# Output projection by seven products of quarters, its combined weight quarters made ready during the second segment

## The chip, the cores and the metric

The kernel runs on one core of a Trainium2 chip. The metric is the device time of one execution in microseconds (us); the times shown are those of three runs, and one more execution was profiled. The core's engines are called PE (matrix products, with PEld for its weight loads), DVE (vector), ACT (scalar and activation), POOL (GpSimd) and SP (here only the queue that issues transfers).

## The reference, cut to what matters

One layer: the input is normalised, multiplied by one wide input matrix, run through four branches (a gated convolution, gated linear attention, pooling windows, a state-space branch), the branches' outputs are set side by side as `mix` (2048 x 1024), and the layer ends with the part that is changed here:

```python
mix = jnp.concatenate([y_a, y_b, y_c, y_d], axis=-1)
x = x + mix @ w_out[layer]            # (2048 x 1024) @ (1024 x 1024)
...
return _rmsnorm(x, final_norm_w)
```

## The kernel before

The 2048 tokens are worked in two segments of 1024 (loop over `s`). Each segment computes its blocks of the input projection, the branches, and writes `mix`, transposed, to a scratch tensor `yd` in device memory (16 token tiles of 128 tokens, each 128 x 8 x 128). Every product is formed from split operands: `split` (L139, L140) makes a rounded high part on ACT and the remainder, the low part, on DVE; `mm3` (L186 to L188) then adds three products, high x low, high x high and low x high, over eight slices of the inner dimension, so one 128 x 512 output takes 24 matmuls. Accumulators come from a ring of three PSUM banks (`acc`), with two more banks tagged `up`.

The output projection follows the second segment. `load_wo` loads and splits the two column halves of the output matrix, half 0 during the last pooling blocks and half 1 at the start of the projection. Then, for each of the 16 token tiles, `load_y` loads a tile of `yd` and the residual input `xk` and splits the tile, `project` computes one column half in 24 matmuls, adds the residual on DVE (L796), and squares the sum on ACT for the row's mean square (L797; L799 and L801 gather it), and `emit` runs the reciprocal root on DVE (`rsqrt`, L127 to L135), scales the row by it and by the norm weight (L807), and stores it (L808). The last tile's second half is done in two pieces of 256 columns, and its output in three pieces, so that less is left to do when PE ends.

All transfers are issued by SP, one queue in program order; each issue waits in place until its buffer is free and its source is ready. The order of the instructions on each engine is set by the framework's scheduler; code that is queued with `later(n, fn)` is written out n blocks later, in `step()`.

Of the kernel before, what the change touches and what calls it, by code (L numbers as in the profile page):

```python
# [52 lines left out]
@with_exitstack  # L53
def tile_hybrid_trunk(ctx: ExitStack, tc: tile.TileContext, xtok, xT, wkv, wch, wpu, wz, wo, pw_, nw, par, gw, fnw, out):
    nc = tc.nc
    vec, act, pe, sp = nc.vector, nc.scalar, nc.tensor, nc.sync
# [207 lines left out]
    def later(n, fn):  # L264

        queue.append([n, fn])
# [246 lines left out]
    wout = []

    def load_wo(n):
        hi, lo = big(n)
        for i in range(4):
            raw = pw.tile([P, 2, 512], F32, tag="raw", name=nm("raw"), bufs=3)
            sp.dma_start(raw, wo[n, i])
            split(raw, hi[:, 2 * i:2 * i + 2, :], lo[:, 2 * i:2 * i + 2, :])  # L520
        wout.append((hi, lo))

# [78 lines left out]
    for s in range(NSEG):  # L601
# [170 lines left out]
    tiles = {}

    def load_y(tt):
        yr = pw.tile([P, KD, P], F32, tag="raw", name=nm("yr"), bufs=3)
        sp.dma_start(yr, yd[tt])
        yh = pw.tile([P, KD, P], F32R, tag="wh", name=nm("yh"))
        yl = pw.tile([P, KD, P], F32R, tag="wl", name=nm("yl"))
        split(yr, yh, yl)
        xk = px.tile([P, D], F32, tag="xtok", name=nm("xk"))  # L780
        sp.dma_start(xk, xtok[tt])
        r = px.tile([P, D], F32, tag="xT", name=nm("r"))
        ot = pseg.tile([P, D], F32, tag=("q", "kt")[tt % 2], name=nm("ot"))
        sq = psm.tile([P, 4], F32, tag="sq", name=nm("sq"))
        tiles[tt] = (yh, yl, xk, r, ot, sq)

    def project(tt, c0, c1, i):

        yh, yl, xk, r, ot, sq = tiles[tt]
        hi, lo = wout[c0 // 512]  # L790
        wc = slice(c0 % 512, c0 % 512 + c1 - c0)
        cs = slice(c0, c1)
        o = acc()[:, :c1 - c0]
        mm3(o, [(yh[:, k, :], yl[:, k, :], hi[:, k, wc], lo[:, k, wc]) for k in range(KD)])
        step()
        vec.tensor_tensor(r[:, cs], o, xk[:, cs], ALU.add)  # L796
        act.activation(xk[:, cs], r[:, cs], AF.Square, accum_out=sq[:, i:i + 1])  # L797
# [14 lines left out]
    load_wo(1)
    for n in range(2):
        for tt in range(2):
            project(tt, n * 512, (n + 1) * 512, n)
            if n == 1:
                emit(tt)
    for tt in range(2, NTT):
        load_y(tt)
        for i, (c0, c1) in enumerate(((0, 512), (512, 1024)) if tt < NTT - 1 else ((0, 512), (512, 768), (768, 1024))):  # L820
            project(tt, c0, c1, i)
        emit(tt)


def _pack(x, norm_w, w_in, conv_a_w, gla_gate_w, gla_gate_b, gla_norm_w, pool_w, pool_scale, ssd_conv_w, ssd_conv_b,
          ssd_dt_bias, ssd_a_log, ssd_d, ssd_norm_w, w_out, final_norm_w):

    f = np.float32
    c = np.ascontiguousarray
    x0 = np.asarray(x)[0]  # L830
    a = {}
    a['xtok'] = c(x0.reshape(SEQ // P, P, D))
    a['xT'] = c(x0.reshape(SEQ // HALF, HALF, KD, P).transpose(0, 3, 2, 1))
    w = np.asarray(w_in)[0]
# [7 lines left out]
    a['wo'] = c(np.asarray(w_out)[0].reshape(4, 2, P, 2, 512).transpose(3, 0, 2, 1, 4))  # L842
# [58 lines left out]
```

## Time and profile before

| | us |
|---|---|
| median of 3 runs (lowest, highest) | 828.62 (828.38, 830.47) |
| the profiled execution | 828.5 |
| its span, first to last instruction | 826.7 |
| PE busy in the span | 815.3 |
| DVE busy in the span | 499.2 |
| ACT busy in the span | 277.2 |
| POOL busy in the span | 3.1 |

The span is what the trace covers; 1.8 us of the profiled execution lie outside it. PE is busy for 99% of the span at a granted clock of 0.996, so times on the other engines count only where PE waits for them, and behind PE's last matmul.

### The profile page before, as it was taken

The numbers are of one execution on the slowest core, as the hardware profiler recorded it, in microseconds if no ns is written. First come the engines' busy times: TensorE is split into PE (matmuls) and PEld (weight loads), VectorE is DVE, ScalarE is ACT, GpSimd is POOL, SyncE is SP. The second block draws the span as 40 slices with busy tenths as digits, with TensorE's granted clock in tenths as the row PEclk, the third lists the DMA queues.
The fourth block names the chain that finished last, engine by engine and source line by source line (L and its number), as shares of the span: only waits on it lengthen the run. The fifth ranks groups of instructions, "written<-read, shape, count | busy, mean of one in ns | idle before, by whom it ended". The sixth has DMA issues, their size and how long they took to land.

```text
span 826.7 us, 11204 instructions
## 1 busy us (share of the span) xinstructions
PE 815.3 (99%) x4304; PEld 676.9 (82%) x4304; DVE 499.2 (60%) x1253; ACT 277.2 (34%) x491; POOL 3.1 (0%) x18
## 2 busy tenths in 40 slices
PE   8999999999999999999999999999999999999996
PEld 7988888787878888998888778788888888888885
DVE  6678576665554679946555453643668665545544
ACT  5755442341222413445454111122323422221211
POOL 0000000000000000000000000000000000000000
PEclk9999999999999999999999999999999999999999
DMA  8840210353330324430111011120146553343221
GB/s 280 320 154 25 77 52 26 107 191 119 92 88 1 122 74 146 147 103 27 52 51 52 27 58 45 52 62 16 55 157 198 177 184 134 142 153 128 102 102 52
DMA packets 38133, 85.66 MB, mean 104 GB/s; under 512 B 3680, under 2 KB 17344, under 8 KB 38080
## 3 DMA queue, kind: packets, MB, share of 16 engines
q1 hardware_dynamic: 38080, 84.95, 30.7%
q8 instruction: 34, 0.56, 0.3%
q14 instruction: 19, 0.16, 0.1%
HBM read 67.11 MB, written 17.83 MB: 103 GB/s over the span
## 4 chain that ended last, share of the span: by engine, by line
PE 97%; DMA 1%; DVE 1%; SPq 0%; ACT 0%; issue 0%; DVEq 0%; ACTq 0%
PE acc L186 30%; PE acc L188 29%; PE acc L187 29%; PE up L398 1%; PE oy L406 1%; PE up L581 1%; PE tr L649 1%; PE oy L410 1%; PE acc L581 1%; DMA xT<-in_xT 1%; DMA raw<-in_wkv 1%; PE oy L581 1%; PE up L394 1%; PE tr L166 0%; PE tr L211 0%; PE tr L708 0%
## 5 line engine op out<-in xcount | busy, mean ns | idle before, releaser
L186 PE MATMUL acc<-bl,wh 128*128 128x512 f32 x640 | 253.8, 397 | 0.0
L188 PE MATMUL acc<-bh,wl 128*128 128x512 f32 x640 | 249.8, 390 | 0.0
L187 PE MATMUL acc<-bh,wh 128*128 128x512 f32 x640 | 249.4, 390 | 0.0
L188 PEld LDWEIGHTS acc<-bh,wl 128*128 128x128 f32 x640 | 120.1, 188 | 25.5
L186 PEld LDWEIGHTS acc<-bl,wh 128*128 128x128 f32 x640 | 120.2, 188 | 25.1
L187 PEld LDWEIGHTS acc<-bh,wh 128*128 128x128 f32 x640 | 120.3, 188 | 23.6
L187 PE MATMUL acc<-bh,yh 128*128 128x512 f32 (+1 forms) x264 | 101.0, 383 | 0.0
L188 PE MATMUL acc<-bh,yl 128*128 128x512 f32 (+1 forms) x264 | 101.0, 383 | 0.0
L186 PE MATMUL acc<-bl,yh 128*128 128x512 f32 (+1 forms) x264 | 101.0, 383 | 0.0
L139 ACT CAST wh<-raw 128x1024 fp32r<-128x1024 f32 (+3 forms) x57 | 55.8, 980 | 121.8 <-PE acc L187 112.9
L140 DVE TENSOR_TENSOR wl<-raw,wh 128x1024 fp32r<-128x1024 f32 (+3 forms) x57 | 64.5, 1134 | 39.0 <-ACT wh L139 35.8
L186 PE MATMUL acc<-wl,bh 128*128 128x512 f32 (+1 forms) x192 | 69.1, 360 | 0.0
L188 PE MATMUL acc<-wh,bl 128*128 128x512 f32 (+1 forms) x192 | 68.4, 356 | 0.0
L187 PE MATMUL acc<-wh,bh 128*128 128x512 f32 (+1 forms) x192 | 68.4, 356 | 0.0
L383 DVE SCALAR_TENSOR_TENSOR g<-g,prm,g 128x512 f32<-128x512 f32 x72 | 53.6, 749 | 6.7 <-ACT g L381 5.2
L187 PEld LDWEIGHTS acc<-bh,yh 128*128 128x128 f32 x264 | 49.6, 188 | 9.8
L186 PEld LDWEIGHTS acc<-bl,yh 128*128 128x128 f32 x264 | 49.6, 188 | 9.7
L188 PEld LDWEIGHTS acc<-bh,yl 128*128 128x128 f32 x264 | 49.6, 188 | 9.6
L796 DVE TENSOR_TENSOR r<-acc,xk 128x512 f32<-128x512 f32 (+1 forms) x33 | 22.3, 675 | 57.1 <-PE acc L188 55.8
L797 ACT ACTIVATE xk<-r 128x512 f32<-128x512 f32 (+1 forms) x33 | 20.3, 616 | 87.0 <-issue 66.7
L186 PEld LDWEIGHTS acc<-wl,bh 128*128 128x128 f32 x192 | 36.1, 188 | 5.2 <-issue 0.3
L188 PEld LDWEIGHTS acc<-wh,bl 128*128 128x128 f32 x192 | 36.1, 188 | 5.1
(195 smaller groups left out, 880.7 us busy)
## 6 DMA issues: line engine op xcount, KB each, us to landing
raw<-in_wch SPq DMA_DIRECT2D x36, 512.0 KB, 3.4
xk<-in_xtok SPq DMA_DIRECT2D x24, 512.0 KB, 3.7
yr<-yd SPq DMA_DIRECT2D x16, 512.0 KB, 4.2
out<-ot SPq DMA_DIRECT2D x30, 256.0 KB, 2.4
xT<-in_xT SPq DMA_DIRECT2D x14, 512.0 KB, 4.6
xtok<-in_xtok SPq DMA_DIRECT2D x8, 512.0 KB, 4.6
raw<-in_wz SPq DMA_DIRECT2D x8, 512.0 KB, 3.8
yd<-g SPq DMA_DIRECT2D x16, 256.0 KB, 3.0
```

The lines of the kernel that those rows point to most:

```text
L139: act.copy(hi, raw)
L140: vec.tensor_sub(lo, raw, hi.bitcast(F32))
L186: pe.matmul(o, lhsT=lh, rhs=rl, start=i == 0, stop=False)
L187: pe.matmul(o, lhsT=lh, rhs=rh, start=False, stop=False)
L188: pe.matmul(o, lhsT=ll, rhs=rh, start=False, stop=i == last)
L383: vec.scalar_tensor_tensor(t, xin[:, k:k + 512], pcol('scw', 4 * i + k), t, ALU.mult, ALU.add)
L394: pe.matmul(o[h * 32:(h + 1) * 32, 0:CH], lhsT=kt[r, tt, h * 32:(h + 1) * 32], rhs=kv[r, tt, h * CH:(h + 1) * CH], start=True, stop=True)
L398: pe.matmul(o[:, CH + g * P:CH + (g + 1) * P], lhsT=bt[r, tt, g, :], rhs=wxs[r, tt, g * P:(g + 1) * P], start=True, stop=True)
L406: pe.matmul(oy[rows[i], 0:256], lhsT=q[:, tok[i]], rhs=st[i][0], start=True, stop=True)
L581: pe.matmul(o[tt][:, :KVN], lhsT=a[:, k, sl], rhs=wk[0][k][b], start=k == 0 and i == 0, stop=k == KD - 1 and i == 2)
L796: vec.tensor_tensor(r[:, cs], o, xk[:, cs], ALU.add)
L797: act.activation(xk[:, cs], r[:, cs], AF.Square, accum_out=sq[:, i:i + 1])
```

## The change

The 16 token tiles are taken in eight pairs. A pair's left factor is cut into four quarters (two token tiles by two halves of the inner dimension), the output matrix too (two halves of the inner dimension by two column halves), and the pair's four 128 x 512 outputs are formed from seven products of quarters in place of eight, with sums of quarters as factors. A product takes 12 matmuls of 512 columns (`mm12`).

- **Weights.** `wout_sums` forms four combined weight quarters on DVE, in place, and stores them to a scratch tensor `td`. `wq_load` loads each of the seven weight quarters (four from `td`) and splits it; b11, t2, b21, t1 and t3 go into segment tiles that are free by then and into the buffers of the first half of the input, t4 and b22 into those of the second half while the first pair is computed.
- **Left factors.** `prep7` splits seven quarters for each pair and forms the four sums s1 to s4 on POOL. It is advanced by one step behind each product.
- **Products and outputs.** `first7` forms a = a11 b11; `second7` puts its negative into a second accumulator b on ACT; `pair7` adds the other six products to a, b and a bank e, and reads b out twice on the way (`cp2`, `cp3`). The seven are, in PE's order, a11 b11 (ahead of the pair), s2 t2, a12 b21, s1 t1, s3 t3, a22 t4 and s4 b22; the next pair's a11 b11 stands between s3 t3 and a22 t4.
- **Order.** From the projection on, every engine keeps the order of the program text (`Ordered`, `strict`).

```diff
+    def wout_sums(g):
...
+            vec.tensor_sub(b11, b11, b12)
+            vec.tensor_sub(b12, b12, b22)
+            vec.tensor_add(b22, b22, b11)
+            vec.tensor_sub(b21, b21, b22)
+            for i, x in enumerate((b11, b22, b12, b21)):
+                sp.dma_start(td[i, :, 2 * g:2 * g + 2, :], x)
+        later(1, go)
+    def wq_load(n, hi, lo):
...
+        for g in range(2):
+            raw = px.tile([P, 2, HALF], F32, tag="xtok", name=nm("wq"))
+            sp.dma_start(raw, src[:, 2 * g:2 * g + 2, :])
+            split(raw, hi[g], lo[g])
+            yield 1
+    def prep7(raw, w7, n=0):
+        a11, a12, a21, a22, s1, s2 = raw
...
+        put('a11', a11)
+        pool.tensor_add(s1, a21, a22)
+        pool.tensor_add(s2, s1, a11)
+        pool.tensor_add(a21, a21, a11)
+        yield 1
+        put('a12', a12)
+        yield 1
+        put('s2', s2)
+        pool.tensor_add(s2, s2, a12)
+        yield 1
+        for n, r in (('s1', s1), ('s3', a21), ('a22', a22), ('s4', s2)):
+            put(n, r)
+            yield 1
+    def second7():
+        b = acc()
+        act.activation(b, ahead[0][0], AF.Copy, scale=-1.0)
+        ahead[0][1] = b
+    def pair7(w7, ev11, ev21, d12, d22, cp2, cp3, done, after=None):
+        a, b = ahead[0]
+        mm12(b, w7['s2'], Hw['t2'], False)
+        cp2(d12, b)
+        tick()
+        mm12(a, w7['a12'], Hw['b21'], False)
+        ev11(a)
+        tick()
+        e = ps_up.tile([P, 512], F32, tag="up", name=nm("e"))
+        mm12(e, w7['s1'], Hw['t1'], True)
+        tick()
+        mm12(b, w7['s3'], Hw['t3'], False)
+        cp3(d22, b)
+        vec.tensor_sub(d22, d22, e)
+        done(0)
+        tick()
+        if after is not None:
+            after()
+            tick()
+        mm12(b, w7['a22'], Hw['t4'], False)
+        if after is not None:
+            second7()
+        ev21(b)
+        done(1)
+        tick()
+        mm12(e, w7['s4'], Hw['b22'], False)
+        vec.tensor_sub(d12, e, d12)
+        done(2)
+        tick()
...
+            if j == 0:
+                later(1, lambda: square(self.r[1][1], self.sq[1], 0))
+            elif j == 1:
+                later(2, lambda: emit(self.tt + 1, self.rows[1], self.sq[1]))
+            else:
+                later(1, lambda: square(self.r[0][1], self.sq[0], 1))
+                later(3 if self.tt + 2 < NTT else 1, lambda: emit(self.tt, self.rows[0], self.sq[0]))
```

PE up to the start of the projection keeps its order. The first rows of the projection before are groups of 24 (here the heads of the first two; `yh`, `yl` are a token tile's parts, `bh`, `bl` the matrix half's):

```order
L186 MATMUL acc_5636<-bl_5444,yh_5598 128x512 [waits DVE_49,Activation_49]
L187 MATMUL acc_5636<-bh_5443,yh_5598 128x512
L188 MATMUL acc_5636<-bh_5443,yl_5599 128x512 [waits DVE_49]
...
L186 MATMUL acc_5664<-bl_5444,yh_5609 128x512 [waits Activation_49]
L187 MATMUL acc_5664<-bh_5443,yh_5609 128x512
```

After the change these are PE's rows of the last two pairs, the head of each product: the end of the pair of tiles 12 and 13 (acc_6691 is its b, e_6785 its e, acc_6832 the next pair's a), then the pair 14 and 15 (acc_6859 is its b, e_6944 its e):

```order
L75 MATMUL acc_6832<-wq_5258,wh_5581 128x512 [waits Activation_49]
...
L75 MATMUL acc_6691<-bh_5694,wh_5736 128x512 [waits DVE_49]
...
L75 MATMUL e_6785<-bl_5695,wh_5581 128x512 [waits DVE_49]
...
L75 MATMUL acc_6859<-wq_5487,wh_5590 128x512 [waits Activation_49]
...
L75 MATMUL acc_6832<-bh_5491,wh_5590 128x512 x2
...
L75 MATMUL e_6944<-bl_5492,wh_5696 128x512 x2
...
L75 MATMUL acc_6859<-wq_5490,wh_5696 128x512 [waits DVE_49,Activation_49]
...
L75 MATMUL acc_6859<-bh_5694,wh_5736 128x512 [waits DVE_49,Activation_49]
...
L75 MATMUL e_6944<-bl_5695,wh_5736 128x512 [waits DVE_49,Activation_49]
```

The pair 12 and 13 has the next pair's product ahead of a22 t4 (the second head); in the last pair a22 t4 (the last head but one) follows s3 t3 directly, on the same bank b, which DVE reads between the two.

DVE in a middle pair, from the last product of the pair of tiles 0 and 1 (r_5721 and r_5722 are its rows) to `cp3`, the second reading of b (acc_5851) in the pair 2 and 3; the splits write `wl`:

```order
L75 TENSOR_TENSOR r_5721<-e_5769,r_5721 128x512 [waits PE_49]
L75 TENSOR_TENSOR wl_5697<-raw_5575,wh_5696 128x512 [waits DMAHW4_49,Activation_49]
L75 TENSOR_SCALAR na_5875<-sq_5689 128x1 [waits DVE_49]
...
L75 SCALAR_TENSOR_TENSOR r_5722<-r_5722,ny_5874,g_5691 128x512
L75 SCALAR_TENSOR_TENSOR sq_5688<-sq_5688 128x1 [waits Activation_49]
L75 SCALAR_TENSOR_TENSOR r_5893<-acc_5851,g_5794 128x512 [waits DMAHW0_49,PE_49]
L75 TENSOR_TENSOR wl_5697<-raw_5580,wh_5696 128x512 [waits Activation_49]
L75 TENSOR_TENSOR r_5893<-acc_5824,g_5788 128x512 [waits DMAHW7_49,PE_49]
L75 TENSOR_TENSOR wl_5737<-raw_5574,wh_5736 128x512 [waits DMAHW4_49,Activation_49]
L75 TENSOR_SCALAR na_5931<-sq_5688 128x1 [waits DVE_49]
...
L75 SCALAR_TENSOR_TENSOR r_5721<-r_5721,ny_5930,g_5691 128x512
L75 TENSOR_TENSOR wl_5737<-raw_5574,wh_5736 128x512 [waits DMAHW5_49,Activation_49]
L75 TENSOR_TENSOR r_5894<-acc_5851,g_5794 128x512 [waits DMAHW2_49,PE_49]
```

Two whole tiles are emitted between the two ends, and four splits.

The end of DVE's program, before:

```order
L796 TENSOR_TENSOR r_6837<-acc_6896,xk_6835 128x256 [waits PE_49]
L801 SCALAR_TENSOR_TENSOR sq_6839<-sq_6839 128x1 [waits Activation_49]
L127 TENSOR_SCALAR na_6925<-sq_6839 128x1 [waits DVE_49]
...
L807 SCALAR_TENSOR_TENSOR ot_6838<-r_6837,ny_6924,fw 128x384 [waits DMAHW7_49,DMAHW0_49,DVE_49]
L807 SCALAR_TENSOR_TENSOR ot_6838<-r_6837,ny_6924,fw 128x320 x2
```

and after (r_6898 is tile 15's row, r_6897 tile 14's):

```order
L75 TENSOR_TENSOR r_6897<-e_6944,r_6897 128x512 [waits PE_49]
L75 TENSOR_SCALAR na_7006<-sq_6809 128x1 [waits DVE_49]
...
L75 SCALAR_TENSOR_TENSOR r_6898<-r_6898,ny_7005,g_5690 128x512 [waits DVE_49]
L75 SCALAR_TENSOR_TENSOR r_6898<-r_6898,ny_7005,g_5691 128x512
L75 SCALAR_TENSOR_TENSOR sq_6808<-sq_6808 128x1 [waits Activation_49]
L75 TENSOR_SCALAR na_7021<-sq_6808 128x1 [waits DVE_49]
...
L75 SCALAR_TENSOR_TENSOR r_6897<-r_6897,ny_7020,g_5690 128x512 [waits DVE_49]
L75 SCALAR_TENSOR_TENSOR r_6897<-r_6897,ny_7020,g_5691 128x512
```

One whole tile is emitted behind the last product before the last row's own emission.

## Rows read from the trace of the kernel before

**Rows 1.** The page: busy time of each engine, and the chain that ended last.
```profile
PE 815.3 (99%) x4304; PEld 676.9 (82%) x4304; DVE 499.2 (60%) x1253; ACT 277.2 (34%) x491; POOL 3.1 (0%) x18
PE 97%; DMA 1%; DVE 1%; SPq 0%; ACT 0%; issue 0%; DVEq 0%; ACTq 0%
```

**Rows 2.** Busy time by stretch: pooling blocks, projection, end (columns as headed).
```profile
core 0: us, PE busy (x) PEld busy (x) DVE busy (x) ACT busy (x) POOL busy (x), PEclk, DMA share, GB/s
600.00:645.00 45.00, 45.00 (x208) 37.41 (x207) 35.11 (x72) 13.70 (x22) 0.00 (x0) 1.00 0.51 164
644.78:819.30 174.52, 174.52 (x793) 145.34 (x791) 91.66 (x234) 40.70 (x83) 0.00 (x0) 1.00 0.38 134
819.30:826.70 7.40, 0.03 (x1) 0.00 (x0) 3.57 (x13) 0.51 (x2) 0.00 (x0) 0.80 0.20 71
```

**Rows 3.** Timeline of PE: a group's end and the next's start; 256-column matmuls.
```profile
698.96 0.39 PE L188 MATMUL acc<-bh,yl 128*128 128x512 f32 x1
699.18 0.39 PE L186 MATMUL acc<-bl,yh 128*128 128x512 f32 x1
...
813.42 0.28 PE L186 MATMUL acc<-bl,yh 128*128 128x256 f32 x1
813.54 0.28 PE L187 MATMUL acc<-bh,yh 128*128 128x256 f32 x1
```

**Rows 4.** Timeline behind that group: residual, square, and one tile's emission.
```profile
699.38 0.69 DVE L796 TENSOR_TENSOR r<-acc,xk 128x512 f32<-128x512 f32 x1 [3.76 <-PE acc L188]
700.12 0.63 ACT L797 ACTIVATE xk<-r 128x512 f32<-128x512 f32 x1
...
701.38 0.15 DVE L801 SCALAR_TENSOR_TENSOR sq<-sq 128x1 f32<-128x1 f32 x1
701.57 0.15 DVE L127 TENSOR_SCALAR na<-sq 128x1 int32<-128x1 int32 x1
...
703.30 1.41 DVE L807 SCALAR_TENSOR_TENSOR ot<-r,ny,fw 128x512 f32<-128x512 f32 x2
```

**Rows 5.** Groups by form: half splits, copies out of PSUM, POOL's largest.
```profile
L140 DVE TENSOR_TENSOR bl<-hf,bh 128x512 fp32r<-128x512 f32 x16 | 10.8, 687 | 0.8 <-ACT bh L139 0.7
L139 ACT CAST bh<-hf 128x512 fp32r<-128x512 f32 x16 | 9.9, 621 | 17.0 <-DVE hf L259 16.8
L381 ACT ACTIVATE g<-acc,prm 128x512 f32<-128x512 f32 x12 | 9.4, 784 | 0.0
L222 ACT COPY g<-acc 128x512 f32<-128x512 f32 x20 | 11.6, 582 | 20.9 <-PE acc L188 17.4 <-issue 3.6
L305 POOL MEMSET rst<- 96x512 f32 x4 | 2.0, 522 | 325.3 <-DVE g L499 323.0 <-DVE g L509 2.3
```

**Rows 6.** Timeline of the end.
```profile
819.37 0.42 DVE L796 TENSOR_TENSOR r<-acc,xk 128x256 f32<-128x256 f32 x1 [1.72 <-PE acc L188]
822.29 1.54 DVE L807 SCALAR_TENSOR_TENSOR ot<-r,ny,fw 128x384 f32<-128x384 f32 x3
```

**Rows 7.** Transfers: issues, KB of each, median us from issue to landing.
```profile
raw<-in_wo SPq DMA_DIRECT2D x8, 512.0 KB, 3.7
out<-ot SPq DMA_DIRECT2D x30, 256.0 KB, 2.4
out<-ot SPq DMA_DIRECT2D x2, 160.0 KB, 1.9
```

**Rows 8.** Groups of the projection: a whole weight split on ACT and DVE.
```profile
L139 ACT CAST bh<-raw 128x1024 fp32r<-128x1024 f32 x8 | 8.2, 1049 | 13.4 <-PE acc L186 8.4 <-DMA raw<-in_wo 4.9
L140 DVE TENSOR_TENSOR bl<-raw,bh 128x1024 fp32r<-128x1024 f32 x8 | 9.6, 1221 | 1.3 <-ACT bh L139 1.2
```

**Rows 9.** Timeline of DVE at the start of the second segment.
```profile
353.01 0.68 DVE L307 TENSOR_TENSOR rst<-tr,rst 16x512 fp32r<-16x512 f32 x1 [1.89 <-ACT rst L306]
360.75 2.38 DVE L140 TENSOR_TENSOR wl<-raw,wh 128x1024 fp32r<-128x1024 f32 x2 [7.06 <-ACT wh L139]
...
373.09 0.17 DVE L379 COPY halo_x<-g 128x3 f32<-128x3 f32 x1 [2.47 <-ACT g L222]
379.29 1.23 DVE L140 TENSOR_TENSOR wl<-raw,wh 128x1024 fp32r<-128x1024 f32 x1 [2.68 <-ACT wh L139]
```

More of the change, by code (lines that the diff above doesn't have):

```diff
@@ L21 @@
 KD = D // P
+KH = KD // 2
 CH = 64
@@ L55, in tile_hybrid_trunk, with __init__, __getattr__, call @@
     nc = tc.nc
-    vec, act, pe, sp = nc.vector, nc.scalar, nc.tensor, nc.sync
+    strict = [False]
+    class Ordered:
+        def __init__(self, eng):
+            self.eng, self.last = eng, None
+        def __getattr__(self, name):
+            def call(*args, **kw):
+                f = getattr(self.eng, name)
+                if not strict[0]:
+                    self.last = None
+                    return f(*args, **kw)
+                if self.last is None:
+                    r = f(*args, **kw)
+                else:
+                    with tc.issue_after(self.last):
+                        r = f(*args, **kw)
+                self.last = r.ins
+                return r
+            return call
+    vec, act, pe, sp, pool = [Ordered(e) for e in (nc.vector, nc.scalar, nc.tensor, nc.sync, nc.gpsimd)]
     cp = ctx.enter_context(tc.tile_pool(name="cp", bufs=1))
@@ L511, in pool_z, with go @@
         spill(s, f, 4 + j, sz)
[L513 to L521, printed above, removed]
+    Hw = {}
+    prep_, side = [None], [None]
+    def wout_sums(g):
+        t = {}
+        for q, tag in (((0, 0), "xT"), ((1, 0), "xT"), ((0, 1), "xtok"), ((1, 1), "xtok")):
+            t[q] = px.tile([P, 2, HALF], F32, tag=tag, name=nm("wo"))
+            sp.dma_start(t[q], wo[q[0], q[1], :, 2 * g:2 * g + 2, :])
+        def go():
+            b11, b12, b21, b22 = t[0, 0], t[1, 0], t[0, 1], t[1, 1]
+            vec.tensor_sub(b11, b11, b12)
[5 more added lines that the diff above has]
+        later(1, go)
@@ new lines, in tile_hybrid_trunk, with slot, load7 @@
+    rings = dict(wh=[0, [], F32R, 4], wl=[0, [], F32R, 4], raw=[0, [], F32, 3])
+    def slot(tag):
+        r = rings[tag]
+        i, n = r[0], r[3]
+        r[0] += 1
+        if i < 2 * n and i % 2 == 0:
+            r[1].append(pw.tile([P, 1024], r[2], tag=tag, name=nm(tag), bufs=n))
+        return r[1][i // 2 % n][:, i % 2 * 512:(i % 2 + 1) * 512]
+    def load7(tt):
+        raw = [slot("raw") for _ in range(4)]
+        for t, (a, b) in ((tt, raw[0:2]), (tt + 1, raw[2:4])):
+            sp.dma_start(a, yd[t][:, 0:KH, :].rearrange("p k n -> p (k n)"))
+            sp.dma_start(b, yd[t][:, KH:KD, :].rearrange("p k n -> p (k n)"))
+        return raw + [slot("raw") for _ in range(2)]
@@ new lines, in prep7, with put @@
+    def prep7(raw, w7, n=0):
+        a11, a12, a21, a22, s1, s2 = raw
+        def put(n, r):
+            w7[n] = slot("wh"), slot("wl")
+            split(r, *w7[n])
+        for _ in range(n):
+            yield 1
[11 more added lines that the diff above has]
+            put(n, r)
+            yield 1
@@ new lines, in tick, with chain, mm12 @@
+    def tick():
+        for g in (prep_, side):
+            if g[0] is not None and next(g[0], 0) == 0:
+                g[0] = None
+        step()
+    def chain(*gs):
+        for g in gs:
+            yield from g
+    def mm12(o, w, h, start):
+        (wh, wl), (hh, hl) = w, h
+        for k in range(KH):
+            ks = slice(k * P, (k + 1) * P)
+            for i, (a, b) in enumerate(((wh, hl), (wh, hh), (wl, hh))):
+                pe.matmul(o, lhsT=a[:, ks], rhs=b[k], start=start and k == 0 and i == 0,
+                          stop=k == KH - 1 and i == 2, skip_group_check=True)
@@ new lines, in tile_hybrid_trunk, with first7 @@
+    ahead = [None]
+    def first7(w7):
+        a = acc()
+        mm12(a, w7['a11'], Hw['b11'], True)
+        ahead[0] = [a, None]
+    def second7():
[31 more added lines that the diff above has]
+        tick()
@@ L764, in tile_hybrid_trunk, with store, square @@
                 pool_z(s, j, f, block_ch(f, wp[j][1]), ab)
+                if f == 1 and s + 1 == NSEG:
+                    for _ in range(4):
+                        next(rest)
+                    if j == 0:
+                        w7 = {}
+                        prep_[0] = prep7(load7(0), w7)
+                        for _ in range(4):
+                            next(prep_[0])
                 if f == 1 and s + 1 < NSEG:
                     wk[0] = load_kv((0, 1)) if j == 0 else wk[0] + load_kv((2,))
-    fw = pseg.tile([P, D], F32, tag="kv", name="fw")
-    sp.dma_start(fw, fnw.to_broadcast([P, D]))
-    vec.tensor_single_scalar(fw, fw, 1.0 / RS, ALU.mult)
+    while queue:
+        step()
     NTT = SEQ // P
[L772 to L797, printed above, removed]
+    def store(dst, src):
+        later(1, lambda: sp.dma_start(dst, src))
+    def square(r, sq, i):
+        junk = px.tile([P, HALF], F32, tag="hf", name=nm("junk"))
+        act.activation(junk, r, AF.Square, accum_out=sq[:, i:i + 1])
         if i == 0:
@@ L812, in tile_hybrid_trunk @@
[L812 to L822, printed above, removed]
+        for c in range(2):
+            cs = slice(c * 512, (c + 1) * 512)
+            vec.scalar_tensor_tensor(r[:, cs], r[:, cs], rs, fw[c], ALU.mult, ALU.mult)
+            store(out[tt, :, cs], r[:, cs])
@@ new lines, in tile_hybrid_trunk @@
+    rows = Rows(0)
+    fw = [gen()[:, :512] for _ in range(2)]
+    for c in range(2):
+        sp.dma_start(fw[c], fnw[:, c * 512:(c + 1) * 512].to_broadcast([P, 512]))
+    q5 = big(1)
+    strict[0] = True
+    next(prep_[0])
+    next(prep_[0])
+    side[0] = chain(wq_load('t4', halves(q5[0][:, 0:4, :]), halves(q5[0][:, 4:8, :])),
+                    wq_load('b22', halves(q5[1][:, 0:4, :]), halves(q5[1][:, 4:8, :])))
+    later(4, lambda: [act.activation(t, t, AF.Copy, scale=1.0 / RS) for t in fw])
@@ new lines, in tile_hybrid_trunk @@
+    first7(w7)
+    second7()
+    for tt in range(0, NTT, 2):
+        w_next = {}
+        nxt = []
+        if tt + 2 < NTT:
+            prep_[0] = chain(prep_[0] or (), prep7(load7(tt + 2), w_next))
+            later(3, lambda: nxt.append(Rows(tt + 2)))
+        rows.take()
+        pair7(w7, rows.ev11, rows.ev21, rows.r[0][1], rows.r[1][1], rows.cp2, rows.cp3, rows.done,
+              after=(lambda: first7(w_next)) if tt + 2 < NTT else None)
+        w7 = w_next
+        rows = nxt[0] if nxt else None
@@ L825, in _pack @@
+    while queue:
+        tick()
 def _pack(x, norm_w, w_in, conv_a_w, gla_gate_w, gla_gate_b, gla_norm_w, pool_w, pool_scale, ssd_conv_w, ssd_conv_b,
```

62 lines of the change are left out of this document (52 added, 10 removed).

## The prediction, on record before the result

> **What bounds the kernel now.** I read the page first: PE is busy for 815.3 of 826.7 us, and the chain that ended last is PE for 97% [rows 1]. So I looked at the stretch the change touches, by windows: from 644.78 to 819.30, the whole output projection, PE is busy without a gap at full clock while DVE works 91.7 us and ACT 40.7 [rows 2]. There the other engines have room, and what counts is how many matmuls PE issues and at what spacing. The timeline gives the spacing by starts, not by the 0.39 us that each row lasts (they overlap): 698.96 to 699.18, and 0.12 us for the 256-column ones [rows 3]. The projection has 31 groups of 24 wide matmuls (744) and two of 24 narrow ones (48 x 0.12 = 5.8), so a wide one takes (174.5 - 5.8) / 744 = 0.2268 us. Last I read what follows PE's last matmul: 7.40 us [rows 2], of which 2.87 lie behind the last vector operation (822.29 + 1.54 = 823.83) [rows 6].
>
> **The matmuls removed.** Eight pairs of seven products of 12 matmuls are 672 wide ones: 672 x 0.2268 = 152.4 against 174.5, **-22.1 us**. A product takes 2.72 us and a pair 19.05. The number of columns and the spacing stay, so this is the firmest term.
>
> **Can DVE and ACT feed it?** A pair now asks DVE for 7 splits, 6 readings of PSUM or of e and 4 scalings, 17 operations of about 0.69, and two short chains: 11.7 + 2 x 1.73 + some 0.6 = 15.8 of 19.05 us. A chain and its two scalings take 703.30 - 701.57 = 1.73 and 1.41, so 3.14 [rows 4], a half split 0.69 [rows 5]. The sum fits, but DVE keeps the program's order now, so I follow the dangerous stretch: from the end of s4 b22 (call it 0) to `cp3`, behind which a22 t4 waits. DVE starts 0.20 us behind PE (699.18 to 699.38 [rows 3, 4]); then e's reading, the a22 split, one emission, `cp2`, the s4 split, the reading of a, the next a11 split, another emission, the a12 split, `cp3`: 8 x 0.69 + 2 x 3.14 + 2 x 0.19 (from L801's start to L127's) = 12.2. It ends at 12.4 (it may not begin before s3 t3 ends, 10.9, which it does not). PE wants bank b at 5 x 2.72 = 13.6, since the next pair's a11 b11 covers one product. **1.1 us to spare**, a price of 0 without disturbance. If that product were not between, as in the last pair, the same wait is open: 0.20 + 0.69 + some 0.06 (DVE's 0.69 from 699.38 ends at 700.07, ACT follows at 700.12 [rows 4]) = **+0.95**, once. `cp2` has two products of cover, the e bank likewise, each split at least one. ACT does 7 casts of 0.62, a copy of 0.58 [rows 5] and 4 squares of 0.63 [rows 4] with their sums in a pair, under 9 us.
>
> **POOL's adds.** No row before has POOL adding. The nearest is a memset of 512 columns, 0.52, which only writes [rows 5]. Below I take 0.52; above, three such passes (two read, one written), 1.57; I take two passes, 1.05, since an addition must at least read both. Their results are wanted a product or more later, so their own time costs nothing; they could only cost by holding DVE up. Three of the four fall into the stretch above (the fourth waits for the s2 split, which stands behind `cp3`). I laid them beside DVE's list at 1.05: a22 of the next pair is loaded behind its slot's split (1.6) and lands some 3 us later, so s1 runs from 4.7 and keeps the s4 split (due at 5.5) waiting 0.2; s2 follows that split and delays the a11 split by 0.4; s3 delays the emission's two-input operations by 0.6. That is 1.2 against 1.1 to spare: 0.1 in each of six middle pairs, **+0.5** rounded up. Ends: 0, and 3 x 1.57 - 1.1 = 3.6 a pair, 22.
> The Trainium skill speaks against placing them there: its page "SBUF — State Buffer", section "Who interferes with whom", says a VectorE instruction with two SBUF inputs contends with a GpSimd instruction that reads SBUF, by an exclusive lock held for the whole instruction. Without that rule the term is 0, with it the 0.5 above or more; no run so far shows it.
>
> **The start.** `second7` is new: s2 t2 adds to b, which ACT copies from a, and nothing stands between. 0.20 to ACT, the copy 0.58 (L222; with a scale up to 0.78 [rows 5]), 0.06 back: **+0.9** (0.8 to 1.1).
> In the 45 us before it DVE works 35.1 [rows 2]. The change takes out six whole splits and the norm weight's scaling (6 x 1.22 + 0.7 = 8.0) and puts in eight whole and six half ones (9.8 + 4.1 = 13.9): 41 of 45, so it may arrive late by a few us; s2 t2 ends 3.6 us into the projection plus 2.7, which is DVE's room. The queue is tighter: each weight quarter goes through two raw buffers, load 3.7 [rows 7], cast 1.05, low part 1.22 [rows 8], so two slices every 6.0 us; t4 and b22 are loaded behind a `mix` store that waits for DVE's last pooling operation, and are wanted 17 and 20 us into the projection, two rounds (12) plus that wait (4 to 5). **+0.5**, from 0 to 4.
>
> **The weight sums.** Eight DVE operations of 1.22 (9.8 us) and eight loads, eight stores in SP's queue ahead of the second segment's weights. By the order they come right behind the input's splits, where DVE is idle for 7.06 + 1.89 us until 360.75, and again for 2.47 and 2.68 until 379.29 [rows 9]: 14.1 us of cover, and the second group's waits for the stores sit in the same gaps. SP's next weight load slips by some 1.5 us, three blocks ahead of its use. Price 0; without that cover PE would wait for the gate's products, at most 2.
>
> **The end.** The last pair's tile 15 is emitted behind the last product and ahead of tile 14's own emission, and nothing is cut into pieces any more. From PE's end: 0.20 + 0.69 (e's reading) + 3.14 (tile 15) + 0.19 + 3.14 (tile 14) = 7.36 to the last scaling; then 2.87 as before, and 0.5 more because the last store has 256 KB (2.4) where it had 160 (1.9) [rows 7]: 10.7 against 7.4, **+3.3**.
>
> **Sum.** -22.1 + 0.95 + 0.5 + 0.9 + 0.5 + 3.3 = -15.95. The profiled execution took 828.5 (span 826.7 and 1.8 around it), the median is 828.62, so the two agree: 828.5 - 16.0 = **812.5 us**, the span 810.7. With the small terms at their low ends 811.3, with the tail half a microsecond shorter 810.8.
>
> **The rivals.**
> - *POOL holds DVE up.* For it: every split, every scaling and the emission's small operations read two SBUF tensors, and only 1.1 us are spare. Against it: four of the ten large operations in the stretch read PSUM, and POOL may as well be the one that waits. With 1.57 per add and about two of three felt, 3.3 - 1.1 = 2.2 a pair, six pairs: +13, so 825; with half of that 818.
> - *The projection starts starved.* A quarter or a row of x lands late because SP is held by the last pooling store, and PE waits within the first pair. Two rounds of 3 us late: 816 to 818. For it: DVE at 41 of 45. Against it: the quarters are wanted one by one, 2.72 us apart.
> - *Slower than before.* The same lock, where it decides: 828.6 + 2.5 is 18.6 above the forecast, 3.1 per middle pair, so DVE must lose 4.2 in each. Three adds do that if each blocks DVE for its whole length and takes 1.4 us or more. Then about 832.
> - *No change.* The seven products are there in PE's rows, so it would need stalls of just 16 us; nothing singles that out.
>
> **How the numbers follow.** Forecast as summed (810.5 to 815): 0.60. POOL's hold at 815 to 825: 0.18. Starved start, 814 to 819: 0.12. Slower: 0.06. Within the noise: 0.04. Two and a half us (0.3%) is about what a measurement tells from no change. The range 810.5 to 820 holds the forecast, the start and somewhat over half of POOL's case, 0.82. Faster is 0.60 + 0.18 + 0.12, less 0.01 for the top of POOL's case: 0.89; same 0.05; slower 0.06.
>
> **What would show it.** PE's wide matmuls in the projection: 672, 0.227 apart, about 155 us from first to last. The window of a middle pair: 19.05 us, PE without idle. A gap of 0.8 to 1.1 behind the first 12 matmuls and one of 0.95 ahead of the last pair's a22 t4. A wait of PE on DVE's second reading of b in every pair would be POOL's hold, with half splits longer than 0.69 or late beside POOL's rows. Waits on `wq` splits in the first 25 us would be the starved start. Behind PE's last matmul, 10.7 us. What would make me wrong: POOL's add far over 1.05, or a wait that the order forces and the chain above lacks.

## The result, and the profile after

The changed kernel takes **820.67 us** (median of three, 819.61 to 821.82) against 828.62: a ratio of 0.990, 95% interval 0.987 to 0.993. It is faster, by 8 us where 16 were forecast, and lies above the range (810.5 to 820). The profiled execution (821.8, span 820.0) is the slowest of the three; the forecast span was 810.7, so 9.3 us are to be found.

The page of the changed kernel, its busy times and the chain that ended last (compare [rows 1]):

```profile
PE 800.2 (98%) x4184; PEld 659.9 (80%) x4184; DVE 558.8 (68%) x1319; ACT 301.2 (37%) x545; POOL 49.5 (6%) x50
PE 86%; DVE 8%; DMA 3%; issue 2%; ACT 0%; SPq 0%; DVEq 0%; ACTq 0%
```

PE lost 15 us of work, and DVE now stands in the chain with 8% and transfers with 3%: the chain leaves PE somewhere. The windows say where (against [rows 2]; the first row is the start of the second segment, where the weight sums stand, the last is the end):

```profile
350.00:400.00 50.00, 50.00 (x270) 43.15 (x270) 38.20 (x72) 27.35 (x46) 0.00 (x0) 1.00 0.62 221
...
600.00:645.00 45.00, 45.00 (x208) 37.43 (x207) 39.68 (x72) 17.00 (x27) 5.50 (x4) 1.00 0.48 154
645.30:809.79 164.49, 157.93 (x673) 126.99 (x671) 133.58 (x282) 57.83 (x127) 40.89 (x28) 0.98 0.47 156
667.10:672.40 5.30, 5.22 (x12) 4.13 (x13) 3.76 (x6) 4.18 (x8) 1.28 (x1) 0.50 0.32 121
809.79:820.00 10.21, 0.00 (x0) 0.00 (x0) 6.38 (x22) 0.72 (x2) 0.00 (x0) 0.62 0.27 103
```

The projection lasts 164.5 us where 672 matmuls need 152.4, and for 5.3 us of it PE ran at half clock. PE's timeline shows the breaks (a row "x2" holds two matmuls, started 0.227 apart):

```profile
648.91 0.73 PE L75 MATMUL acc<-wq,wh 128*128 128x512 f32 x2 [0.73 <-ACT acc L75]
...
667.18 1.22 PE L75 MATMUL acc<-bh,wh 128*128 128x512 f32 x2 [4.33 <-DVE r L75]
668.20 0.63 PE L75 MATMUL acc<-bh,wl 128*128 128x512 f32 x1
...
708.10 0.39 PE L75 MATMUL acc<-wq,wl 128*128 128x512 f32 x1
708.59 0.73 PE L75 MATMUL acc<-bh,wh 128*128 128x512 f32 x2
709.17 0.39 PE L75 MATMUL acc<-bh,wl 128*128 128x512 f32 x1
...
804.06 0.70 PE L75 MATMUL acc<-bh,wh 128*128 128x512 f32 x2 [0.88 <-DVE r L75]
```

Every break but the first is ahead of a22 t4 (`acc<-bh,wh`). In the first pair its product starts 4.48 us late and then takes 5.26 in place of 2.72, as the granted clock fell to 0.50 behind the wait: 7.0 us together. In each of the six middle pairs it starts 0.26 late and its third matmul 0.12 (708.10 to 708.59 to 709.17, where 0.227 and 0.453 are usual): 0.38, too little to show as idle time, since a row lasts longer than its spacing. In the last pair 1.13.

So the 9.3 us by the prediction's terms, measured less forecast: the start's copy 1.01 - 0.9 = +0.1; **the starved start 7.0 - 0.5 = +6.5**; **POOL's hold 2.3 - 0.5 = +1.8**; the last pair 1.13 - 0.95 = +0.2; the spacing +0.6 (two or three products of a pair take 2.74 to 2.75 for 2.72); the end 10.2 - 10.7 = -0.5. With +0.5 for the head, as PE reaches the projection at 645.30 where it did at 644.78 (in the profiles shown here, between 644.85 and 647.14), 9.2.

**The first pair**, in rows of SP, ACT and DVE:

```profile
652.60 0.38 SPq L70 DMA_DIRECT2D yd<-g  x1
653.02 0.99 SPq L70 DMA_DIRECT2D g<-in_xtok  x2
654.06 0.92 SPq L70 DMA_DIRECT2D g<-in_fnw  x2
655.02 0.43 SPq L75 DMA_DIRECT2D wq<-td  x1
```
```profile
662.15 1.05 ACT L75 CAST bh<-wq 128x1024 fp32r<-128x1024 f32 x1 [8.61 <-DMA wq<-td]
```
```profile
663.23 1.23 DVE L75 TENSOR_TENSOR bh<-wq,bh 128x1024 fp32r<-128x1024 f32 x1 [5.79 <-ACT bh L75]
...
665.31 1.22 DVE L75 TENSOR_TENSOR bl<-wq,bl 128x1024 fp32r<-128x1024 f32 x1 [0.19 <-ACT bl L75]
666.45 0.68 DVE L75 TENSOR_TENSOR r<-acc,g 128x512 f32<-128x512 f32 x1
```

SP can't issue the last pooling store before 652.60; t4's second slice stands behind it and is cast only at 662.15, seven us after its issue. DVE, bound to the program's order, idles 5.79 us for it, and `cp3` (666.45) stands behind that split and b22's. s3 t3 had ended at 660.1 and the next pair's a11 b11 at 662.9, so bank b and PE wait for a reading that had itself been ready for 6 us. t4's own split ends at 664.46: for the quarter alone PE would have waited 1.8 of the 4.48 us at most, an estimate from these rows.

**A middle pair**, POOL's and DVE's rows in the stretch that the prediction followed:

```profile
698.94 1.43 POOL L75 TENSOR_TENSOR raw<-raw 128x512 f32<-128x512 f32 x1 [7.19 <-DMA raw<-yd]
701.72 3.00 POOL L75 TENSOR_TENSOR raw<-raw,raw 128x512 f32<-128x512 f32 x2 [1.35 <-issue]
```
```profile
699.13 1.25 DVE L75 SCALAR_TENSOR_TENSOR sq<-sq 128x1 f32<-128x1 f32 x1
...
701.50 0.68 DVE L75 TENSOR_TENSOR r<-acc,g 128x512 f32<-128x512 f32 x1
702.11 1.46 DVE L75 TENSOR_TENSOR wl<-raw,wh 128x512 fp32r<-128x512 f32 x1
703.49 0.14 DVE L75 TENSOR_SCALAR na<-sq 128x1 int32<-128x1 int32 x1
...
703.85 0.88 DVE L75 SCALAR_TENSOR_TENSOR na<-ny,sq 128x1 f32<-128x1 f32 x1
...
707.86 0.68 DVE L75 TENSOR_TENSOR r<-acc,g 128x512 f32<-128x512 f32 x1
```

A sum of one column takes 1.25 in place of 0.15 [rows 4] and ends with POOL's addition (700.37); the split takes 1.46 in place of 0.69; the next one-column operation with two tensors (703.85) takes 0.88 where its like take 0.22, and ends with POOL's third addition (704.72), 0.66 late. Between them a reading from PSUM and an operation with one tensor keep their 0.68 and 0.14. The hold is 1.10 + 0.77 + 0.66 = 2.53 us a pair ahead of `cp3`. Over the projection, by groups (busy us, mean ns), a half split has 838 ns for the 687 of [rows 5], and an addition 1485:

```profile
L75 DVE TENSOR_TENSOR wl<-raw,wh 128x512 fp32r<-128x512 f32 x51 | 42.7, 838 | 2.5 <-ACT wh L75 2.5
...
L75 POOL TENSOR_TENSOR raw<-raw,raw 128x512 f32<-128x512 f32 x21 | 30.9, 1485 | 52.2 <-DVE wl L75 41.3 <-issue 10.9
```

### The profile page after: what moved, and what is told of

Read it like the earlier page. It is cut to its first block, busy times and chain, and to the rows that moved or that the text cites. A ratio compares the mean times of both kernels' runs of the same rounds, so it can differ in the third digit from the quotient of the medians.

```text
span 820.0 us, 11262 instructions
## 1 busy us (share of the span) xinstructions
PE 800.2 (98%) x4184; PEld 659.9 (80%) x4184; DVE 558.8 (68%) x1319; ACT 301.2 (37%) x545; POOL 49.5 (6%) x50
## 4 chain that ended last, share of the span: by engine, by line
PE 86%; DVE 8%; DMA 3%; issue 2%; ACT 0%; SPq 0%; DVEq 0%; ACTq 0%
PE acc L70 68%; PE acc L75 5%; PE up L70 3%; PE tr L70 3%; PE e L75 3%; PE oy L70 3%; DVE r L75 3%; DVE wl L75 2%; DMA raw<-yd 2%; DVE na L75 1%; DVE sq L75 1%; DMA wq<-td 1%; DVE ny L75 1%; DMA xT<-in_xT 1%; SPq L70 0%
## 5 line engine op out<-in xcount | busy, mean ns | idle before, releaser
L70 PE MATMUL acc<-bh,wh 128*128 128x512 f32 x640 | 249.4, 390 | 0.0
L70 ACT CAST wh<-raw 128x1024 fp32r<-128x1024 f32 (+4 forms) x61 | 58.1, 956 | 115.8 <-PE acc L70 109.9
L70 DVE SCALAR_TENSOR_TENSOR g<-g,prm,g 128x512 f32<-128x512 f32 (+1 forms) x120 | 90.4, 756 | 10.1 <-ACT g L70 7.6
L70 DVE TENSOR_TENSOR wl<-raw,wh 128x1024 fp32r<-128x1024 f32 (+4 forms) x61 | 67.1, 1105 | 27.4 <-ACT wh L70 24.2
L75 PE MATMUL acc<-wq,wh 128*128 128x512 f32 x191 | 59.2, 391 | 0.7 <-ACT acc L75 0.7
L75 ACT ACTIVATE junk<-r 128x512 f32<-128x512 f32 x32 | 20.2, 632 | 91.5 <-DVE r L75 85.2
L75 PE MATMUL acc<-bh,wh 128*128 128x512 f32 x128 | 42.2, 412 | 5.8 <-DVE r L75 5.2
L70 PEld LDWEIGHTS acc<-wh,bh 128*128 128x128 f32 x208 | 39.5, 190 | 6.4 <-ACT wh L70 1.4
L75 DVE TENSOR_TENSOR wl<-raw,wh 128x512 fp32r<-128x512 f32 x51 | 42.7, 838 | 2.5 <-ACT wh L75 2.5
L70 DVE TENSOR_TENSOR g<-acc,rb 128x512 f32<-128x512 f32 x28 | 19.3, 688 | 35.4 <-PE acc L70 35.4
L75 PEld LDWEIGHTS acc<-wq,wh 128*128 128x128 f32 x191 | 35.8, 188 | 8.8 <-ACT acc L75 1.2
```

Of the source, the lines that this page charges most:

```text
L70: return f(*args, **kw)
L75: r = f(*args, **kw)
```

## The experiments

Each kernel is the changed one with the edit shown. The ratio is to the kernel before, run on the same chip (its medians 828.66 to 829.03); "projection" is from the first product to the end of the last in the profile, 164.49 for the change itself. The profile is of one of a kernel's three or four runs, which spread by 1.4 to 5.5 us, so a loss read from it need not be the median's. By the times alone only e7 and e9 stand clear of the change, with intervals that don't touch its own; the other readings rest on the gaps in PE's rows.

| kernel | us | ratio, 95% interval | projection | first pair and what it drags | a middle pair |
|---|---|---|---|---|---|
| the change | 820.67 | 0.990 (0.987, 0.993) | 164.49 | 7.0 | 0.38 |
| e1 late store | 818.53 | 0.987 (0.986, 0.989) | 160.10 | 1.9 + 0.6 | 0.4 |
| e2 no POOL | 817.90 | 0.988 (0.986, 0.990) | 158.85 | 3.2 + 0.6 | 0 |
| e3 emission later | 823.37 | 0.993 (0.992, 0.995) | 166.47 | 6.7 | 0.77 |
| e4 free order | 816.76 | 0.985 (0.984, 0.987) | 160.73 | 0 (copy: 4.3) | 0.4 (mean) |
| e5 emission behind | 818.68 | 0.988 (0.986, 0.990) | 160.12 | 5.0 | 0 |
| e6 adds on DVE | 817.56 | 0.986 (0.985, 0.988) | 160.39 | 5.3 | 0 |
| e7 early loads | 815.23 | 0.984 (0.982, 0.985) | 158.16 | 0.3 | 0.4 |
| e8 swap | 819.83 | 0.989 (0.987, 0.992) | 163.25 | 9.4 | 0 |
| e9 all | **808.75** | 0.976 (0.975, 0.977) | 153.77 | 0.7 | 0 |
| e10 POOL copies | 817.32 | 0.986 (0.985, 0.988) | 159.54 | 4.4 | 0 |
| e11 POOL fills | 816.96 | 0.986 (0.983, 0.988) | 160.18 | 5.1 | 0 |

**e1, the late store.**

```diff
-        spill(s, f, 4 + j, sz)
+        if s + 1 == NSEG and f == 1 and j == 1:
+            last_spill.append(lambda: spill(s, f, 4 + j, sz))
+        else:
+            spill(s, f, 4 + j, sz)
...
+    later(5, last_spill[0])
     first7(w7)
```

> The last pooling block's store is issued behind the loads of t4 and b22; nothing else changes. Theory 1 (the first pair's 7 us come from SP's queue: t4's second slice is issued only at 655.02, behind that store, and lands at 662): the slice is then issued some 4 us earlier, the 4.5 us wait ahead of the first pair's a22 t4 goes, and with it the half clock behind it (2.5): 813.5 to 815.5. Rival 1 (the transfer is slow because the queues are full there, DMA share 0.83, wherever it stands): 1 to 3 us back at most, 818 to 820. Rival 2 (DVE's order alone, cp3 behind the t4 split, whatever the load does): no change, 820.7. The middle pairs stay at 19.45 in all of them.

t4's second slice is issued and cast 4 us earlier:

```profile
651.11 0.53 SPq L75 DMA_DIRECT2D wq<-td  x1
```
```profile
658.05 1.05 ACT L75 CAST bh<-wq 128x1024 fp32r<-128x1024 f32 x1 [4.18 <-DMA wq<-td]
```

The first pair's wait falls from 4.48 to 1.74, and the clock stays up, so 5.1 of its 7.0 us are back; 0.6 more than usual is lost in the second pair. The projection is 4.4 us shorter, the median 2.1 only: the profiled execution is the quickest of these runs, and that of the change its slowest. Rival 2 falls: the load's place matters. But the median misses theory 1's 813.5 to 815.5 and lies in rival 1's range, and rival 1 has a part in it: the slice still lands seven us after its issue. For the last 1.9, `cp3` also still stands behind b22's first split.

**e2, no additions on POOL.**

```diff
-        pool.tensor_add(s1, a21, a22)
-        pool.tensor_add(s2, s1, a11)
-        pool.tensor_add(a21, a21, a11)
+        if not strict[0]:
+            pool.memset(s1, 0.5)
+            pool.memset(s2, 0.5)
...
-        pool.tensor_add(s2, s2, a12)
```

> The four sums of each pair's left quarters are left out: s1, s2 and s4 are split from a constant and s3 from a21 alone, so the output differs; every split, product and transfer stays, only POOL's additions go. Theory (POOL holds DVE up, 2.5 us a pair in the stretch ahead of cp3, of which 0.4 reaches PE): a22 t4's product returns from 3.11 to 2.72 in six pairs, 2.3 us less, and the half splits all take 0.69; the first pair's wait stays: about 818. Rival (DVE's list is too long by itself, the extra is in the scalings and readings): the pairs stay at 19.45, 820.7. A third reading, that POOL also causes the first pair's wait by holding DVE or SP: then 812 to 814.

PE has no gap from 690 to 790, and DVE shows how much room it had:

```profile
690.00:790.00 100.00, 100.00 (x442) 82.59 (x441) 74.28 (x198) 37.53 (x86) 0.00 (x0) 1.00 0.45 153
```
```profile
691.58 0.69 DVE L75 TENSOR_TENSOR r<-e,r 128x512 f32<-128x512 f32 x1 [1.02 <-PE e L75]
...
701.43 0.69 DVE L75 TENSOR_TENSOR wl<-raw,wh 128x512 fp32r<-128x512 f32 x1
702.48 0.69 DVE L75 TENSOR_TENSOR r<-acc,g 128x512 f32<-128x512 f32 x1 [0.37 <-PE acc L75]
```

DVE is through ahead of `cp3` 10.5 us after it begins and waits 0.37 for PE. The hold of 2.53 less the 0.38 that PE sees leaves a list with about 2.15 to spare, not 1.1: its rows last 0.69, but the next begins 0.60 behind. Against expectation the first pair gained too, 4.48 to 3.06: the last pooling blocks' four operations take 3.09 where POOL's additions made them 4.01, and t4's second slice is issued 8.56 us into the projection in place of 9.72 and lands 1.4 earlier. POOL thus had a hand in both losses, though in the first pair its share can't be told to a microsecond: see e5.

**e3 and e5, the second emission later.** The change's `later(3 ...)` becomes 4 in e3 and 5 in e5.

> The second emission of each pair moves one product later, behind cp3 in DVE's order; POOL's additions stay. Theory (cp3 is late only by what POOL adds to a list that would else have 2 us to spare): cp3 then runs as soon as s3 t3 ends, a22 t4's product is 2.72 in the middle pairs, 2.3 us less: about 818.4, and the next deadlines (s4's reading of e, the a22 split) hold. Rival (the list is full everywhere, so the wait only moves): a gap of about 0.4 shows up ahead of s4 b22 or of the next pair's s2 t2, total 820 to 821.

The pairs came out worse, and the expectation misread the order: with 4 the emission moves only behind the a12 split and is still ahead of `cp3`. The list is the same, but the third addition now meets a split in place of the emission's small operations:

```profile
702.18 1.45 DVE L75 TENSOR_TENSOR wl<-raw,wh 128x512 fp32r<-128x512 f32 x1
703.56 0.14 DVE L75 TENSOR_SCALAR sq<-sq 128x1 f32<-128x1 f32 x1
703.62 1.72 DVE L75 TENSOR_TENSOR wl<-raw,wh 128x512 fp32r<-128x512 f32 x1
```

A hold of 1.03 for 0.66: the pair's wait goes from 0.38 to 0.77. What stands beside POOL sets the price.

> The second emission of each middle pair moves two products later and now stands behind cp3 and e's reading in DVE's order (one product later, as run before, it still stood ahead of cp3). POOL's additions stay. Theory (cp3 is late because 2.5 us of hold stand ahead of it in a list with 2.1 us to spare): 3.1 us leave the list ahead of cp3, so cp3 runs as s3 t3 ends, and a22 t4's product is 2.72 in six pairs: 2.3 us less than the 820.7 of the change, about 818.4, first pair unchanged. Rival (the list is full everywhere and the wait only moves): the emission now delays b's next reading or the a12 and s2 splits, a gap of 0.3 or more per pair shows up ahead of s4 b22 or s2 t2, 820 to 822.

With 5 it is behind `cp3`: six gaps gone, 818.7 as expected, with POOL's additions as they were. The wait doesn't move on. The first pair, in which the edit changes nothing, was to stay as it was, but waits 3.33 for 4.48: t4's second slice lands 6.0 us after its issue (654.66 to 660.68) where it took 7.1 in the change. A difference of about 1 us between two first pairs is thus no sign of an edit's effect.

**e4, the scheduler's order.** `strict[0] = True` is taken out.

> The rule that every engine keeps the order of the program text from the projection on is taken out; the scheduler orders as before. It places t4's second load ahead of the last pooling store, and the second emission half ahead of cp3 as now. Theory 1 (the first pair's wait is that load's place in SP's queue): the first pair loses at most 1 us instead of 7, 813 to 816. Rival 2 (the wait lies elsewhere): first pair unchanged, 820 or more. For the middle pairs no better order is seen in DVE's list, 19.4 to 19.8.

The first a22 t4 waits for nothing, but PE waits 2.43 us shortly behind the first product, since ACT's copy into b now stands behind three casts, one of them waiting for t4's second slice; the clock falls there too (0.61 in 651.2 to 655.6):

```profile
650.67 0.58 ACT L70 ACTIVATE acc<-acc 128x512 f32<-128x512 f32 x1
```
```profile
651.30 0.86 PE L70 MATMUL acc<-wq,wh 128*128 128x512 f32 x2 [2.43 <-ACT acc L70]
```

So the first pair lost 4.3 where at most 1 was expected, and 816.8 lies just above 813 to 816. The scheduler's order has its own late instruction behind a load; a fixed order as such is not shown to be the fault.

**e6, the sums on DVE.** The four `pool.tensor_add` become `vec.tensor_add`.

> The four sums of each pair are formed on DVE in place of POOL, at the same places of the program; nothing else changes. Theory (an addition on POOL costs DVE its own length, as DVE's two-input operations wait until it ends): DVE's list ahead of cp3 gains three additions of 0.69, 2.1 us, and loses 2.5 of hold, so a22 t4's product is 2.72 in the middle pairs and every half split 0.69: 818 to 819.5. Rival (POOL's additions are a real relief and only badly placed): DVE is longer by 2.8 us a pair and cp3 later by some 1 us, 823 to 828.

DVE does the additions itself and PE has no gap from 690 to 790; 817.6, a little better than expected. DVE's busy time there, e6 first and the change behind it:

```profile
690.00:790.00 100.00, 100.00 (x441) 82.59 (x441) 86.28 (x215) 38.01 (x86) 0.00 (x0) 1.00 0.47 155
```
```profile
690.00:790.00 100.00, 99.47 (x433) 80.56 (x432) 87.27 (x189) 37.15 (x85) 29.95 (x21) 1.00 0.48 156
```

86.28 us against 87.27 with POOL helping: the help cost DVE as much as the work.

**e7, early loads.**

```diff
+                        t4raw = wq_raw('t4', "xT")
...
+    b22raw = wq_raw('b22', "xtok")
     rows = Rows(0)
...
-    side[0] = chain(wq_load('t4', ...), wq_load('b22', ...))
+    side[0] = chain(wq_split('t4', t4raw, ...), wq_split('b22', b22raw, ...))
+    next(side[0])
```

with e1's late store; `wq_raw` is the loading half of `wq_load`, `wq_split` the splitting half.

> On top of the late pooling store: t4's two slices are loaded during the last pooling blocks into buffers of the other tag, b22's two right behind t3's splits, and their splits stand at most one behind each of the first three products, so that cp3 waits for no load. Theory (the whole first-pair wait is loads and splits standing ahead of cp3): the first pair's 1.74 and the second's 0.87 that were left with the late store alone go to 0.4 at most each, 816 to 817. Rival (DVE is simply full in the first 20 us, with last pooling, eight splits and POOL's hold): 1 us or more stays ahead of the first a22 t4, 818 or above.

The first pair's loss is 0.3 us (these rows start 0.43 apart where 0.227 is usual, and the third matmul behind them is 0.1 late), and the 815.2 is 0.8 better than the theory's end:

```profile
662.05 0.39 PE L75 MATMUL acc<-wq,wl 128*128 128x512 f32 x1
662.48 0.73 PE L75 MATMUL acc<-bh,wh 128*128 128x512 f32 x2
```

So nearly all of the 7.0 were loads and splits ahead of `cp3`, with the clock's fall that followed; DVE isn't too full.

**e8, the swap.**

```diff
-        cp3(d22, b)
-        vec.tensor_sub(d22, d22, e)
+        vec.tensor_add(d22, b, d22)
...
-        mm12(b, w7['a22'], Hw['t4'], False)
+        mm12(e, w7['s4'], Hw['b22'], False)
```

and the reverse below; x - e is formed right behind s1 t1, and the two emissions change places with their products.

> s4 b22 goes ahead of a22 t4 in each pair, and DVE reads e before s3 t3 ends in place of after it; so two products (in the last pair one) lie between s3 t3 and the next product on b. Nothing else changes. Theory (the only wait in a middle pair is PE's on cp3): the 0.39 goes in six pairs and the 1.14 of the last pair too, 3.4 us less, and the first pair's wait shrinks by up to a product, 2.7, with its half-clock stretch: 813 to 817. The tail: the last product now ends in b's reading and tile 15's emission, tile 14's is done before, so 1 to 2 us less behind PE's last matmul. Rival (the wait moves to e or to the splits of s4): gaps of 0.3 or more ahead of s4 b22 in each pair, 819 to 821.

Middle and last pairs have no gap left, but b22, loaded last, is now wanted one product earlier, and PE waits twice in the first pair, each time with a fall of the clock behind it:

```profile
668.41 1.22 PE L75 MATMUL e<-bl,wh 128*128 128x512 f32 x2 [3.71 <-DVE bl L75]
673.13 1.22 PE L75 MATMUL e<-bl,wh 128*128 128x512 f32 x2 [1.80 <-DVE bl L75]
```

The expected gain in the first pair turned into a loss of 2.4 in the profile, which is of the slowest of the four runs, and the tail gained nothing: tile 14's emission still stood behind the last reading.

**e9, all together.** e7 and e8, and for the first pair alone s1 t1 ahead of s2 t2; for the last, tile 14's root ahead of the last reading.

```diff
+        if first:
+            e = ps_up.tile([P, 512], F32, tag="up", name=nm("e"))
+            mm12(e, w7['s1'], Hw['t1'], True)
         mm12(b, w7['s2'], Hw['t2'], False)
...
+                    later(1, lambda: root(self.sq[0]))
+                    later(2, lambda: emit(self.tt, self.rows[0], None))
```

> Early loads and late store as before, with s4 b22 ahead of a22 t4; the first pair also takes s1 t1 ahead of s2 t2, so that a product covers ACT's copy into b; and tile 14's root is formed before the last reading, its scalings behind it. POOL's additions stay. From the early loads' 815.2: minus 0.39 in six pairs and 1.13 in the last (as in the swap alone), minus 1.0 for the copy, minus 0.6 for what was left in the first two pairs, minus 1.0 in the tail: 809 to 811, with PE at 0.227 from the first to the last of 672 matmuls, about 153 us. If a deadline that none of the runs so far had shown is hit (splits of s4, reading of e), gaps of 0.3 per pair: 812 to 814.

808.75, just under what was expected and 12 us below the change. The projection and the end:

```profile
645.43:799.20 153.77, 153.59 (x673) 125.68 (x671) 134.35 (x287) 57.65 (x127) 40.50 (x28) 1.00 0.50 158
799.20:808.30 9.10, 0.00 (x0) 0.00 (x0) 5.50 (x18) 0.72 (x2) 0.00 (x0) 0.74 0.30 115
```

POOL still adds, for 40.5 us, and DVE is still held; with two products of cover it costs nothing.

**e10 and e11, what of POOL's work holds DVE.** The additions become copies of one quarter, and fills with a constant; both kernels leave the sums out, as e2 does.

> POOL's four additions are replaced by four copies of one quarter each (the sums are left out, so the output differs): one tensor read in place of two, the same number of POOL rows at the same places. If the hold needs only that POOL reads SBUF, the small operation on three SBUF tensors beside the first copy still takes as long as the copy lasts, and a split beside one is longer than 0.69; with copies shorter than additions, a22 t4's wait of 0.39 goes or shrinks: 817 to 820. If only POOL's two-input additions hold DVE, all half splits take 0.69 and the time is that of no additions, 818.

> POOL's four additions are replaced by four fills with a constant (sums left out, output differs): POOL reads nothing and writes the same four half tiles. If the hold comes from POOL reading, no DVE operation beside a fill is longer than alone and the middle pairs have no gap: about 818. If a write alone holds DVE, operations beside the fills are longer by up to a fill (0.5), still too little for a gap in the middle pairs: also about 818, but the half splits' mean is above 0.69.

A copy and the one-column sum beside it, in e10:

```profile
695.72 0.72 POOL L75 COPY raw<-raw 128x512 f32<-128x512 f32 x1 [9.29 <-DMA raw<-yd]
```
```profile
695.88 0.57 DVE L75 SCALAR_TENSOR_TENSOR sq<-sq 128x1 f32<-128x1 f32 x1
```

The sum ends with the copy. In e11 a split beside two fills takes what it takes alone:

```profile
698.08 0.99 POOL L75 MEMSET raw<- 128x512 f32 x2 [9.79 <-DVE wl L75]
```
```profile
698.54 0.68 DVE L75 TENSOR_TENSOR wl<-raw,wh 128x512 fp32r<-128x512 f32 x1
```

In these runs POOL had to read SBUF to hold DVE; one tensor read was enough, a write alone did nothing (the half splits' mean is 683 ns with fills, 684 with no POOL at all, 692 with the shorter copies, 838 with the additions).

## Why the prediction was wrong

**Matmuls removed: right.** 672 at 0.227; e9, with nothing in the way, does them in 153.8.

**The start: the step that failed, 7.0 us for 0.5 and above its end of 4.** The copy was right (1.01 for 0.9). Of the quarters I wrote that two slices take 6.0 us, that t4 and b22 wait for the pooling store, 4 to 5 us, and are wanted 17 and 20 us in. Three things were missing. The load took 7.1 us from issue to landing, not 3.7 [rows 7] (the DMA engines' share is 0.88 in that stretch, though that this is why wasn't tried). POOL's addition beside the last pooling operations put the store off by 0.9. Above all, I asked when PE needs the quarter, not what stands behind its split on DVE: `cp3` does, and through it bank b. e1 and e7 show that the late loads cause it: with them early the 7.0 become 0.3. That the reading's place behind them makes most of the wait, 2.7 of the 4.48, is read from the change's rows; no run moved `cp3` ahead and left the loads late. On top came the clock, 2.5 of the 7.0, for which the prediction had no term.

**POOL's hold: the right mechanism, mis-sized on both sides, 2.3 us for 0.5.** Hold 2.53 a pair where I had 1.2, room 2.15 where I had 1.1 (my own 13.6 - 12.4 is 1.2). The hold: I took 1.05 for an addition, which lasts 1.48 on average, and let the operations lose parts of it, where each lost what was left of the addition. The room: I added rows at their full length where DVE's next row starts sooner, 0.60 behind one of 0.69 seven times and 0.4 us more in the emissions and their sums, the very trap I had avoided for PE. That both were about half of what they should be keeps the difference small, and that is luck: 0.38 a pair stays where I had 0.1. The rival's 13 us don't appear.
The Trainium skill's rule that I weighed ("SBUF — State Buffer", section "Who interferes with whom") agrees with every row above: operations with two SBUF tensors are held by POOL's additions (1.25 for 0.15) and copies (0.57), not by fills (0.68), and readings from PSUM not at all (0.68). Its page "GPSIMD Engine Reference", section "4.1 Engine selection", puts a two-input elementwise operation there at about twice VectorE's time, so an estimate by it is 2 x 0.69 = 1.38; the trace has 1.48, inside my bounds and above the value that I took.

**The last pair and the end: right.** 1.13 for 0.95, 10.2 for 10.7. **The weight sums: right**, PE is busy for 50.00 us of 350 to 400.

**The rivals.** The starved start and POOL's hold both came true, and I had given them chances as alternatives, each on top of a forecast without the other. By my own figures, 4.5 us for the one (817) and 5.5 or more for the other (818 to 825), the two together would have come out at 822 or above.

## What to carry to other kernels

Where an engine keeps the program's order, ask of every load and split not when its own result is wanted but what stands behind it in that queue, and whose buffer that one frees. An addition on POOL is no relief for a full DVE if both work from SBUF: count it at its full length beside DVE's two-input operations, or give the product that waits one more product of cover, which made the hold free here. Mechanisms that live in different stretches add; they aren't rivals of each other.

## What the runs showed of the hardware

- DVE's operation is held whole, however small: one column, 0.15 alone, took 1.25 beside an addition on POOL.
- The granted clock fell to the lower level (1.2 GHz) behind PE's waits of 4.3 us (the change), 2.7 (e10) and 2.4 (e4), and stayed at the upper one (2.4 GHz) behind 2.9 in e2. So the wait's length alone doesn't sort these cases, and what decides stays open. Where it fell, it cost about 2.5 us in the change, more than half of the wait itself.
- A transfer of 512 KB, 3.7 us at the median in the kernel before [rows 7], took 6.0 (e5) to 7.3 (e6) where the rows of x and the norm weight were loaded just ahead of it, 7.1 in the change.
